# Inverses by blocks of 16 with corrections on TensorE, and 104 weight chunks split during the first feed-forward

## The chip, the cores and the metric

The kernel runs on one core of one Trainium2 chip. The metric is the device time of one execution in microseconds (us). Three executions of the kernel before took 2127.75, 2129.2 and 2129.91 us; the median is 2129.2 us.

## What is computed

One layer of a hybrid decoder for 264 tokens: 256 of a prompt and 8 single tokens of running sequences. D is 2048, the feed-forward width F is 5504.

```python
x = x + 0.5 * swiglu(rmsnorm(x, n1), f1g, f1u, f1d)      # first feed-forward
h = rmsnorm(x, nm)
proj = h @ w_in                                           # 2048 -> 4864 columns
o_att = attend(q, k, v, sinks)                            # 16 heads, window 128, sinks, relative bias
o_rwkv = rwkv_time_mix(proj[..., ATT_COLS:], ...)         # 16 heads of 64
x = x + concatenate([o_att, o_rwkv]) @ w_out
x = x + 0.5 * swiglu(rmsnorm(x, n2), f2g, f2u, f2d)      # second feed-forward
```

The time mixing is a recurrence over tokens with a 64x64 state S per head:

```python
sa = einsum('bhij,bhj->bhi', S, -kk_t)
S = S * exp(lw_t) + sa[..., None] * (kk_t * a_t) + v_t[..., None] * k_t
y_t = einsum('bhij,bhj->bhi', S, r_t)
```

The kernel computes it for the prompt in four chunks of 64 tokens. Within a chunk it needs, for each head, the inverse of a unit triangular 64x64 matrix I - L, with L strictly triangular. 16 heads times 4 chunks make 64 such inverses. All is float32.

## The kernel before

**Weights.** Every large product is computed as three fp32r products. A weight w is split into hi (w rounded to fp32r) and lo = w - hi, the activation likewise; hi·xh, hi·xl and lo·xh are added in PSUM. `gemm` (L126) walks over a product's rows in chunks of four blocks of 128x128. `chunk` (L115) loads a chunk (256 KB) into one of 6 `raw` buffers from SP's queue (L121), rounds it on ScalarE into one of 4 `hi` buffers (L122), and subtracts on VectorE into one of 4 `lo` buffers (L123, recorded as L57); of w_in the chunk with k0 = 8 is subtracted on GpSimd. Then TensorE runs 12 matmuls of 128x128 by 264 (L73, into the PSUM tiles `acc`). A function `step` is called after each chunk.

**Stages.** The first feed-forward has 43 column tiles in six parts; each part runs its gate and up products, then its share of the down product. Its last part writes x to DRAM (`xsp`) and begins the next norm. The mixing stage follows: 38 tiles of w_in (48 matmuls each, 1824 in all, `win`), tiny products between them, then w_out (768 matmuls). The second feed-forward is built like the first. The feed-forwards have 6192 weight matmuls each.

**Small work in the mixing stage.** It is written as Python generators in a list `tasks`; `tick` (the `step` of w_in and w_out) moves each one to its next `yield`. A scheduler then orders the instructions of every engine by its own estimate; SP's queue, ScalarE's and the others each run in the order so written. The generators:

- `prep`, one for each of 8 pairs of heads: decays, normed keys, and the masked products `gm` (L423) that hold L; 8 stores a batch, of 128-byte rows, bring the two diagonal 32x32 blocks of each L to DRAM (`sa`, L426).
- `chain`, one for each of 4 batches of 2 pairs (16 inverses). It loads the 32 diagonal blocks in two forms (`X`, and `Xt`, rows shared out over 4 groups of 32 partitions; L475, L476, 8 transfers), runs 30 elimination steps of two VectorE instructions each (L486, L487), stores the result to DRAM (`sb`, L491, 4 transfers), loads it in its final layout (`TT`, L496, 4 transfers), adds the identity and transposes (L503, L506), and fills the off-diagonal 32x32 block by two rounds of 16 products of 32x32 on TensorE (L513, L524). Then come the products with `kr` (L538), with `W` (L551), the three steps of the state over the chunks (L575 to L592), a group norm and the output gate.
- `attend`, one for each of 8 query tiles: scores, softmax, transposes (L730 to L732), products with v.
- `dec_rwkv`, the recurrence of the 8 single tokens, in 16 slices of four head rows, with GpSimd and VectorE; `dec_attend`, their attention.

**Order of w_out.** `PASS` (L39) gives the passes over the rows of w_out: pairs 0 to 5 of the time mixing first, then the eight attention tiles, then pairs 6 and 7. `need` drains the generators that a pass waits for; any pass with a time-mixing pair also waits for the single tokens' recurrence. In the last pass each finished tile of x is also split and squared for the next norm.

The rules of the buffers: 3 `acc` and 5 `m` tiles in PSUM; TT in 2 buffers, X and Xt in 1 each.

Of the kernel before, what the change touches and what calls it, by code (L numbers as in the profile page):

```python
# [32 lines left out]
DWAIT = (8, 8, 8, 4)  # L33
# [13 lines left out]
def body(tc, I, O):  # L47
# [42 lines left out]
    def pause(n):  # L90
        for _ in range(n):
            yield

    with ExitStack() as ctx:
# [20 lines left out]
        def chunk(src, n, e, ahead=True):  # L115
            w = n * P
            with tc.high_priority() if ahead else nullcontext():
                raw = wp.tile([P, CH * P], F32, tag="raw", bufs=NRAW, name=uid("raw"))
                hi = wp.tile([P, CH * P], F32R, tag="hi", bufs=NHL, name=uid("hi"))
                lo = wp.tile([P, CH * P], F32R, tag="lo", bufs=NHL, name=uid("lo"))  # L120
                SP.dma_start(raw[:, :w], src)  # L121
                A.copy(hi[:, :w], raw[:, :w])  # L122
                tt(e, lo[:, :w], raw[:, :w], hi[:, :w].bitcast(F32), ALU.subtract)  # L123
            return hi, lo

        def gemm(ps, src, xs, step=None, rng=None, pool=False, ahead=True):  # L126
            n = len(xs)
            for k0 in range(0, n, CH):
# [3 lines left out]
                hi, lo = chunk(src[:, k0 * P:k1 * P], k1 - k0, G if pool and k0 in LOP else V, ahead)  # L132
# [6 lines left out]
                if step:  # L139
                    step()  # L140

# [47 lines left out]
        def early(pi):  # L189
            keep = tc.keep_in_program_order  # L190
            if pi == 1:
                keep(A.dma_start(C, I["cst"]))
                keep(A.dma_start(ss, I["shs"]))
            elif pi in (2, 3):
                nm, ck = (("ks", "ck"), ("vs", "cv"))[pi - 2]
                keep(A.dma_start(O[nm][:, 0:127, :], I[ck][:, 1:128, :]))
# [67 lines left out]
        def first_ffn(n2):  # L264
# [11 lines left out]
            with tc.tile_pool(name="f1", bufs=1) as fp:  # L276
                cur[0] = (fp, NH)
                for q in range(4):
# [3 lines left out]
                    xr += [xg[:, j] for j in range(4)]  # L282
                ffn(n1, xr, I["gu1"], I["dn1"], nxt, load)

# [5 lines left out]
        def mixing_body(mx, n2, n3):  # L290
# [27 lines left out]
            scr = [dp.tile([BATCH[b] * 16, 1024], F32, tag=f"sa{b}", name=f"sa{b}") for b in range(nbat)]  # L318
            scr2 = [dp.tile([BATCH[b] * 16, 1024], F32, tag=f"sb{b}", name=f"sb{b}") for b in range(nbat)]
# [3 lines left out]
            def win(t):  # L323
                ps = acc()
                gemm(ps, I["win"][t], n2.xs, tick, pool=True)
# [25 lines left out]
            def prep(p, bt, k, xrr, xk, xv):  # L351
# [64 lines left out]
                for h in range(2):  # L416
# [7 lines left out]
                    for blk in range(2):  # L424
                        x = blk * 32
                        SP.dma_start(  # L426
                            scr[bt.i].rearrange("(h b k c) (s t) -> h b k s c t", h=2, b=2, c=4, s=32)[h, blk, k],
                            gm[h * 64 + x:h * 64 + x + 32, :, x:x + 32])
# [34 lines left out]
            def chain(bt):  # L463
# [3 lines left out]
                nr = n * 16  # L467
                ng = P // nr
                if ng == 3:
                    ng = 2  # L470
                nj = 32 // ng
                X = ring((ng * nr, 32, 32), "X", 1)
                Y = ring((ng * nr, nj, 32), "Xt", 1)
                for g in range(ng):
                    SP.dma_start(X[g * nr:(g + 1) * nr], scr[bt.i].rearrange("r (s t) -> r s t", s=32))  # L475
                    SP.dma_start(Y[g * nr:(g + 1) * nr],  # L476
                                 scr[bt.i].rearrange("r (j g t) -> g r j t", g=ng, t=32)[g])
                TT = ring((P, n * 4, 64), "TT", NTT)
                for h in range(2):
                    G.memset(TT[h * 64 + 32:h * 64 + 64, :, 0:32], 0.0)  # L480
                yield from pause(DWAIT[bt.i])
                for s in range(1, 31):
                    m, w = -(-s // ng), 31 - s
                    t = ring((ng * nr, m, w), "st", 2)
                    shp = (ng * nr, m, w)
                    tt(V, t, bc(X[:, s:s + 1, s + 1:], shp), bc(Y[:, :m, s:s + 1], shp), ALU.mult)  # L486
                    tt(V, Y[:, :m, s + 1:], Y[:, :m, s + 1:], t, ALU.add)  # L487
                    if s % NSTEP == 0:
                        yield
                for g in range(ng):  # L490
                    SP.dma_start(scr2[bt.i].rearrange("r (j g t) -> g r j t", g=ng, t=32)[g], Y[g * nr:(g + 1) * nr])  # L491
                yield from pause(1)
                for h in range(2):
                    for blk in range(2):
                        x = h * 64 + blk * 32
                        SP.dma_start(TT[x:x + 32, :, blk * 32:blk * 32 + 32],  # L496
                                     scr2[bt.i].rearrange("(h b m) (s t) -> h b s m t", h=2, b=2, s=32)[h, blk])
                yield from pause(DWAIT[bt.i])
                for h in range(2):
                    for blk in range(2):  # L500
                        x = h * 64 + blk * 32
                        v = TT[x:x + 32, :, blk * 32:blk * 32 + 32]
                        tt(V, v, v, bc(ident[x:x + 32, x:x + 32].unsqueeze(1), (32, n * 4, 32)), ALU.add)  # L503
# [508 lines left out]
```

## Time and profile before

| what | value |
|---|---|
| median of three executions | 2129.2 us (2127.75 to 2129.91) |
| the profiled execution | 2127.34 us, of which its span is 2125.2 us |
| TensorE busy over the span | 2043.9 us, 96% |
| VectorE, ScalarE, GpSimd busy | 1334.3, 1045.8, 419.5 us |
| moved by DMA | 356.27 MB, mean 168 GB/s |
| split of a chunk: ScalarE round, VectorE subtract | 602 ns, 684 ns (means over all) |
| first matmul of w_in to first of w_out | about 764 to 1244 us |

Times in the profile are counted from the span's start. A busy TensorE is not TensorE at its peak: matmuls overlap, so 166 weight matmuls fit in 20 us at the full clock although one is shown with 286 ns. The best measure of the loss is therefore the number of weight matmuls in a stretch beside 166 per 20 us. "PEclk" is the share of the full TensorE clock that was granted. An idle time is put down to the event that ended it.

### The profile page before, as it was taken

Reading aid. Unit: us, or ns where it says so; the run is one execution under the profiler, and the core shown is the slowest. Engines: PE = TensorE matmul, PEld = TensorE weight load, DVE = VectorE, ACT = ScalarE, POOL = GpSimd, SP = SyncE. Lnnn points to the kernel's source line nnn. Section 1 sums busy time; section 2 is a strip of 40 time slices with the busy share of each in tenths; the row PEclk is TensorE's granted clock in tenths of the full one; section 3 lists DMA queues with packets and bytes.
Section 4 is the critical chain, followed back from the end, with each engine's and each line's share of the span. In section 5 each row is a group of like instructions: output and inputs, shape, how many; then the busy total and the mean of one; then the engine's idle time right before and its main releaser. Section 6 shows DMA issues by size and latency. Waiting matters only on the chain.

```text
span 2125.2 us, 45168 instructions
## 1 busy us (share of the span) xinstructions
PE 2043.9 (96%) x16870; PEld 1995.4 (94%) x16870; DVE 1334.3 (63%) x2551; ACT 1045.8 (49%) x2002; POOL 419.5 (20%) x581
## 2 busy tenths in 40 slices
PE   8999999999999999989996899999999999999997
PEld 8999999999999999888885679899999999999997
DVE  5765555556555677766888646755555565555555
ACT  5644444444444566546542344644444444444445
POOL 0301011010201146533454201220110102011012
PEclk9999999999999999989997579999999999999999
DMA  6565565656555574434343145456555565555554
GB/s 224 176 182 182 175 205 175 207 180 183 181 177 185 185 227 139 122 96 135 112 136 114 41 138 186 156 182 181 181 175 187 177 184 181 177 186 176 186 176 140
DMA packets 227532, 356.27 MB, mean 168 GB/s; under 512 B 42176, under 2 KB 83152, under 8 KB 227280
## 3 DMA queue, kind: packets, MB, share of 16 engines
q1 hardware_dynamic: 221616, 344.72, 51.8%
q10 hardware_dynamic: 5696, 8.66, 1.1%
q8 instruction: 132, 2.16, 0.4%
q14 instruction: 88, 0.72, 0.1%
HBM read 345.15 MB, written 10.21 MB: 167 GB/s over the span
## 4 chain that ended last, share of the span: by engine, by line
PE 86%; DVE 7%; DMA 2%; ACT 1%; issue 1%; POOL 1%; SPq 1%; DVEq 0%; POOLq 0%; ACTq 0%
PE acc L73 79%; PE m L73 6%; DVE lo L57 1%; DMA raw<-in_gu 1%; DVE Xt L57 1%; DVE st L57 1%; ACT L67 1%; DVE ld L57 0%; ACT t L67 0%; DMA sb<-Xt 0%; DVE s L60 0%; DVE t L57 0%; DMA TT<-sb 0%; DVE TT L57 0%; DVE t L64 0%
## 5 line engine op out<-in xcount | busy, mean ns | idle before, releaser
L73 PE MATMUL acc<-s,hi 128*128 128x264 f32 x7072 | 1317.5, 286 | 10.0 <-ACT hi L122 8.3
L57 DVE TENSOR_TENSOR lo<-raw,hi 128x512 fp32r<-128x512 f32 (+1 forms) x1266 | 861.7, 684 | 600.6 <-ACT hi L122 578.7
L122 ACT CAST hi<-raw 128x512 fp32r<-128x512 f32 (+2 forms) x1304 | 780.5, 602 | 909.5 <-PE acc L73 830.6
L73 PEld LDWEIGHTS acc<-s,hi 128*128 128x128 f32 x7072 | 1108.8, 190 | 17.8 <-ACT hi L122 8.5
L73 PE MATMUL acc<-s,lo 128*128 128x264 f32 x3536 | 1016.1, 288 | 12.7 <-DVE lo L57 10.5
L73 PEld LDWEIGHTS acc<-s,lo 128*128 128x128 f32 x3536 | 669.9, 189 | 18.5 <-DVE lo L57 14.1
L73 PE MATMUL acc<-t,hi 128*128 128x264 f32 x2752 | 502.7, 284 | 1.6 <-ACT t L251 1.6
L73 PEld LDWEIGHTS acc<-t,hi 128*128 128x128 f32 x2752 | 426.0, 188 | 1.9 <-ACT t L251 1.8
L57 POOL TENSOR_TENSOR t<-t,t 128x264 f32<-128x264 f32 (+1 forms) x162 | 173.0, 1068 | 1209.6 <-ACT hi L122 897.6
L73 PE MATMUL acc<-t,lo 128*128 128x264 f32 x1376 | 388.2, 284 | 0.0
L73 PEld LDWEIGHTS acc<-t,lo 128*128 128x128 f32 x1376 | 258.2, 188 | 0.0
L57 DVE TENSOR_TENSOR t<-acc,t 128x264 f32<-128x264 f32 x164 | 70.9, 433 | 36.7 <-PE acc L73 36.5
L57 POOL TENSOR_TENSOR s<-s,s 128x264 f32<-128x264 f32 (+1 forms) x56 | 49.5, 886 | 195.8 <-ACT s L67 179.1
L57 POOL TENSOR_TENSOR lo<-raw,hi 128x512 fp32r<-128x512 f32 x38 | 49.7, 1308 | 57.4 <-ACT hi L122 57.2
L67 ACT ACT_TABLE_LOAD x42 | 53.9, 1283 | 1.9 <-PEq L1004 1.2
L60 DVE SCALAR_TENSOR_TENSOR s<-acc,s 128x264 f32<-128x264 f32 x96 | 40.7, 428 | 16.8 <-PE acc L73 16.3
L60 DVE SCALAR_TENSOR_TENSOR x<-acc,x 128x264 f32<-128x264 f32 x96 | 40.6, 427 | 10.9 <-PE acc L73 10.4
L57 DVE TENSOR_TENSOR st<-X,Xt 128x60 f32<-128x60 f32 (+10 forms) x120 | 36.1, 300 | 10.1 <-DMA Xt<-sa 7.4
L67 ACT ACTIVATE t<-t 128x264 f32<-128x264 f32 x94 | 40.0, 425 | 3.3 <-DVE t L57 1.8
L57 DVE TENSOR_TENSOR Xt<-Xt,st 128x60 f32<-128x60 f32 (+10 forms) x120 | 36.7, 305 | 1.7
L251 ACT CAST t<-t 128x264 fp32r<-128x264 f32 x86 | 35.5, 413 | 3.6 <-POOL t L57 2.1
L73 PE MATMUL m<-s,hi 128*128 128x264 f32 x160 | 30.1, 287 | 0.4 <-ACT hi L122 0.4
(209 smaller groups left out, 1116.5 us busy)
## 6 DMA issues: line engine op xcount, KB each, us to landing
raw<-in_gu SPq DMA_DIRECT2D x688, 256.0 KB, 3.2
raw<-in_dn SPq DMA_DIRECT2D x224, 256.0 KB, 2.7
raw<-in_win SPq DMA_DIRECT2D x152, 256.0 KB, 3.2
raw<-in_dn SPq DMA_DIRECT2D x160, 192.0 KB, 2.7
raw<-in_wout SPq DMA_DIRECT2D x48, 256.0 KB, 3.0
raw<-in_wout SPq DMA_DIRECT2D x32, 128.0 KB, 2.4
xsp<-x ACTq DMA_DIRECT2D x16, 132.0 KB, 3.5
s<-xsp SPq DMA_DIRECT2D x16, 132.0 KB, 3.0
```

Of the source, the lines that this page charges most:

```text
L57: return e.tensor_tensor(out=out, in0=a, in1=b, op=op)
L60: return V.scalar_tensor_tensor(out=out, in0=a, scalar=s, in1=b, op0=op0, op1=op1)
L67: return A.activation(out=out, in_=in_, func=f, **k)
L73: TE.matmul(out, lhsT, rhs, start=start, stop=stop, **k)
L122: A.copy(hi[:, :w], raw[:, :w])
L251: A.copy(hi, u)
```

## The change

Three things change.

1. **The inverse by blocks of 16.** `gm` is stored to DRAM as whole 64x64 matrices (256-byte rows, one transfer for each pair and half, 4 a batch). The chain loads only the four 16x16 blocks on the diagonal, 64 blocks on 64 partitions, by one transfer of 64-byte rows; it runs 14 elimination steps, stores the blocks back by one transfer into a scratch that was filled with zeros during the first feed-forward, and loads 64x64 matrices U that hold the block-diagonal inverse. Two corrections on TensorE make the full inverse: with W the transpose, F = 2I - W + (low·W), U becomes F·U, and again (five rounds of 16 products of 64x64 in place of two of 32x32).
2. **Weights split ahead.** During the first feed-forward a side task splits 104 chunks, one for every four chunks of the feed-forward's own: the chunks k0 = 0, 4 and 12 of the 24 time-mixing tiles of w_in (72), and the second chunk of each tile and pass of w_out (32). Each is loaded (256 KB), rounded, subtracted, and stored to DRAM as hi and lo beside each other (512 KB, from ScalarE's queue). In the mixing stage such a chunk is loaded whole (512 KB) straight into a buffer for hi and lo, and neither ScalarE nor VectorE touches it.
3. **The passes of w_out** become two: the eight time-mixing pairs, then the eight attention tiles. hi and lo share one buffer of twice the size, 4 of them, as before.

The core of the diff:

```diff
-DWAIT = (8, 8, 8, 4)
+DWAIT = (4, 4)
+PRE, PREK = range(2, 26), (0, 4, 12)
+PSTEP = 4
-PASS = [[0, 1, 2, 3, 4, 5], [8, 9, 10, 11, 12, 13, 14, 15], [6, 7]]
+PASS = [[0, 1, 2, 3, 4, 5, 6, 7], [8, 9, 10, 11, 12, 13, 14, 15]]
...
-        def chunk(src, n, e, ahead=True):
+        def chunk(src, n, e, ahead=True, done=None):
...
+                hl = wp.tile([P, 2, CH * P], F32R, tag="hl", bufs=NHL, name=uid("hl"))
+                hi, lo = hl[:, 0], hl[:, 1]
+                if done is not None:
+                    SP.dma_start(hl[:, :, :w].bitcast(F32), done)
+                else:
+                    raw = wp.tile([P, CH * P], F32, tag="raw", bufs=NRAW, name=uid("raw"))
+                    SP.dma_start(raw[:, :w], src)
+                    A.copy(hi[:, :w], raw[:, :w])
+                    tt(e, lo[:, :w], raw[:, :w], hi[:, :w].bitcast(F32), ALU.subtract)
...
+        def presplit(fp):
+            todo = [("win", t, k, CH) for t in PRE for k in PREK]
+            k0 = 0
+            for ks in PASS:
+                if len(ks) > CH:
+                    todo += [("wout", o, k0 + CH, len(ks) - CH) for o in range(KD)]
+                k0 += len(ks)
+            for i, (nm, t, k, n) in enumerate(todo):
+                w = n * P
+                raw = fp.tile([P, CH * P], F32, tag="praw", bufs=3, name=uid("praw"))
+                hl = fp.tile([P, 2, CH * P], F32R, tag="phl", bufs=3, name=uid("phl"))
+                tc.keep_in_program_order(SP.dma_start(raw[:, :w], I[nm][t, :, k * P:k * P + w]))
+                A.copy(hl[:, 0, :w], raw[:, :w])
+                tt(V, hl[:, 1, :w], raw[:, :w], hl[:, 0, :w].bitcast(F32), ALU.subtract)
+                d = dp.tile([P, 2, w], F32, tag=f"pre{i}", name=f"pre{i}")
+                A.dma_start(d, hl[:, :, :w].bitcast(F32))
+                ready[nm, t, k] = d
+                yield from pause(PSTEP)
...
+                for g in side:
+                    next(g, None)
...
+                X = ring((nr, 16, 16), "X", 2)
...
+                SP.dma_start(X, diag(scr[bt.i]))
+                yield from pause(DWAIT[0])
+                G.memset(X.rearrange("r s t -> r (s t)")[:, 0:256:17], 1.0)
+                for s in range(1, 15):
+                    w = 15 - s
+                    t = ring((nr, s, w), "st", 2)
+                    tt(V, t, bc(X[:, s:s + 1, s + 1:], (nr, s, w)), bc(X[:, :s, s:s + 1], (nr, s, w)), ALU.mult)
+                    tt(V, X[:, :s, s + 1:], X[:, :s, s + 1:], t, ALU.add)
...
+                SP.dma_start(diag(scr2[bt.i]), X)
...
+                for h in range(2):
+                    SP.dma_start(U[HALF[h]], scr2[bt.i][h * nj:(h + 1) * nj, 0:4096].rearrange("j (s t) -> s j t", s=64))
+                yield from pause(DWAIT[1])
+                V.transpose(W, U)
...
+                for last in (False, True):
+                    ps = times(low, W)
+                    F = square("F", 1)
+                    stt(F, W, -1.0, bc(I2.unsqueeze(1), (P, nj, 64)), ALU.mult, ALU.add)
+                    tt(V, F, ps, F, ALU.add)
+                    yield
+                    pu = times(part(F), U)
+                    if not last:
+                        pw = times(part(U), F)
+                        W = square("Wt", 1)
+                        A.copy(W, pw)
+                    U = square("U")
+                    V.tensor_copy(U, pu) if last else A.copy(U, pu)
+                    yield
+                TT = U
```

Here `low` reads `gm` and `times` runs 16 products of 64x64 by 64 into one PSUM tile. In the changed program's instruction order TensorE's 1824 matmuls of w_in still stand ahead of those of w_out, in the same sequence. What stands between them differs: the first correction product of batch 3 stands behind 1776 of them (before: the first off-diagonal product of batch 3 stood behind all 1824), and behind the last of them stand only the end of the state steps, the group norm, and the same attention products as before.

More of the change, by code (lines that the diff above doesn't have):

```diff
@@ L466, in chain @@
                     yield
[L467 to L487, printed above, removed]
+                nr, nj = n * 32, n * 4
```

94 lines of the change are left out of this document (41 added, 53 removed).

## The prediction

> **What bounds the kernel now.** I read the 40 slices of the page first, then busy times by stage, then TensorE's waits, then its timeline.
>
> ```profile
> PE   8999999999999999989996899999999999999997
> DVE  5765555556555677766888646755555565555555
> PEclk9999999999999999989997579999999999999999
> DMA  6565565656555574434343145456555565555554
> ```
>
> Both feed-forwards are full at full clock; their own work cannot get faster here. All slack is in slices 15 to 26, the mixing stage. By stage (columns: busy us and instructions of PE, its weight loads, DVE, ACT, POOL; granted clock; DMA share; GB/s):
>
> ```profile
> 8.00:14.00 6.00, 5.63 (x30) 5.30 (x31) 3.54 (x7) 2.60 (x6) 0.00 (x0) 1.00 1.03 410
> 100.00:700.00 600.00, 598.22 (x4916) 597.53 (x4915) 345.67 (x587) 281.35 (x495) 61.48 (x57) 1.00 0.58 185
> ...
> 1340.00:1362.00 22.00, 18.70 (x132) 16.48 (x131) 22.00 (x45) 19.23 (x50) 12.01 (x14) 1.00 0.50 160
> ```
>
> ```profile
> 764.00:1147.00 383.00, 354.51 (x3173) 332.06 (x3171) 298.03 (x667) 203.18 (x423) 193.14 (x331) 0.96 0.46 133
> 1147.00:1199.00 52.00, 33.55 (x303) 27.74 (x302) 31.63 (x100) 10.27 (x37) 13.61 (x20) 0.62 0.19 53
> 1199.00:1244.00 45.00, 37.57 (x136) 24.17 (x136) 27.82 (x107) 24.68 (x75) 6.03 (x17) 0.58 0.29 83
> 1244.00:1362.00 118.00, 114.51 (x941) 109.97 (x941) 78.36 (x159) 61.06 (x133) 18.04 (x28) 0.97 0.52 163
> ```
>
> The last weight matmul of w_in starts at 1147, the first of w_out at 1244: 97 us without one. In the first 52 of them batch 3's inverse ends alone, at a clock of 0.62; the other 45 are attention tiles. At 740 to 764 DMA already runs at a share of 0.82 and 241 GB/s beside a full TensorE.
>
> TensorE's waits in 764 to 1147, then in 1147 to 1244:
>
> ```profile
> PE acc L73 <- DVE lo L57: 9.2, 8, 3.1
> PE m L73 <- DVE gm L57: 5.3, 4, 3.1
> ```
>
> ```profile
> PE m L73 <- DVE TN L506: 12.4, 1, 12.4
> PE m L730 <- DVE t L64: 5.0, 3, 2.9
> ```
>
> VectorE is behind all four: 298 of 383 us busy, with the inverses and the weights in one queue.
>
> **The stage 764 to 1147, taken apart.** 166 weight matmuls fit in 20 us, 121 ns each (page, slices at 100%), so w_in's 1824 cost 221. The tiny products cost 104 (sum over the timeline of the time to the next start, less waits). 58 are left: 28 in listed waits, 30 in a low clock and stretched gaps.
>
> **The change, part by part.**
>
> *Splits during the first feed-forward.* 104 subtractions at 684 ns are 71 us of VectorE, 104 roundings at 602 ns and 104 issues at 330 ns (the xsp stores' row) 97 us of ScalarE. They run beside the first 416 of its 536 chunks, 588 us of TensorE. VectorE goes from 58% to 70%, ScalarE from 47% to 63%: hidden by the four chunks that lie ready. DMA is the tight one: those 416 chunks are 105.9 MB, and 104 times 768 KB add 81.8, in all 187.7 MB in 588 us, 319 GB/s. The trace has 410 GB/s at 8 to 14 us, with 2 KB rows on SP's queue beside ScalarE's. So 78% of that: I take no stall there, but +4 us for the start, where loads bind until 16 us and two more of 256 KB stand in SP's queue. Bounds: 0, and +48 if 295 GB/s (752 to 754 us, share 1.00, mixed with xsp stores) is all that DMA gives. The zero fill, 1.1 MB and eight issues, is 3 us of DMA at 410 GB/s and hidden alike.
> The Trainium skill ("DMA: Bandwidth & Descriptors", Specifications) puts the HBM limit of a core at about 358 GB/s; the 410 here is above it, and even at 358 the 319 would pass.
>
> *The chain.* Per batch go 60 steps (72.8 us over four, 18.2 each), 4 additions and 2 transposes (2.9 us), 16 SP transfers of some 0.55 us issue, 8 gm stores. There come 28 steps on 56 elements or fewer: 0.16 us (8 elements) to 0.33 (60), I take 0.25, 7 us; a transpose of 512 elements (two of 256: 0.86), two F operations of 0.69 each twice and one copy (0.6): 4.2 us. TensorE gives back two rounds at 1.04 us for five of 64x64. These are in no row; 48 of that shape by W, below, start within 2.4 us, 0.8 for 16, at most 1.4 like uv,t:
>
> ```profile
> 932.90 0.33 PE L73 MATMUL m<-t,W 64*64 64x64 f32 x2
> ...
> 935.30 1.37 PE L73 MATMUL m<-uv,t 128*64 128x64 f32 x29
> ```
>
> +2 us a batch, bounds 0 and +5. The new transfers of 1024 rows of 64 B: Xt's 1024 rows of 128 B take four issues of 0.56 and land in 2.8, so 5 us there and 5 back; bounds 2.5 and 10 each. From gm to the first correction: gm 0.7, store 2.5, X 5.4, steps 10.5 (half again for what lies between), back 5.1, U 3.2, transpose 0.9: 28 us. In the changed order 178 weight matmuls (21.6) and about 8 us of tiny products stand there, 30 us. So batches 0 to 2 are barely covered; late next are these transfers.
> The Trainium skill (same page, Specifications) says that below 512 B a transfer is read, modified and written; if that doubled the 64-byte stores it would add 5 us a batch, inside my bound of 10, while the 128-byte stores here land in 2.7 us.
>
> *w_in with ready chunks.* 72 of 152 subtractions leave VectorE (796 ns here, 57 us); with the steps (some 45 less) and the 4.2 us items it falls from 298 to about 200 of 380 us. The 9.2 and 5.3 us above go, and most of the clock dips. A new wait comes in: a ready chunk is loaded into one of only 4 buffers, freed three chunks ahead (4.36 us at full rate), where raw had 6 more; SP stops on that buffer with the chain's transfers queued behind it. Landing of 512 KB is not shown: 16 KB land in 2.1 us, 256 KB in 3.2, so 4.3 by that slope plus 0.3 issue; bounds 3.2 and 7.8 (528 KB of x in the crowded start). At 4.6, 0.24 us for each four chunks, hidden in w_in behind the tiny products (some 3 us a tile). Batch 3's inverse and two attention halves move into this stage: 35 us of tiny products at a clock of 0.62 are about 22 at full, and the corrections 8. So 221 + 104 + 30 = 355, plus what is left of 58: I take 30 (bounds 10 and 60). 385 us, +2.
>
> *The tail.* Behind the last w_in matmul now stand two state steps, norm and gate (5 us), and the 45 us of attention, same instructions. What is new there: the single tokens' recurrence starts 210 weight matmuls before the end (before: 326) and needs 16 times four GpSimd operations of 0.8, 52 us, so it ends about 12 us into the tail, on VectorE too: +5. 97 becomes 55, -42 (bounds 40 and 75).
>
> *w_out.* 768 at 121 ns are 93 of 118. The old last pass of two blocks gives 0.73 us of matmul a tile and VectorE 1.5: full for 22 us while TensorE started 132 of 181. With eight blocks, 2.9 us a tile, that 6 us goes. Waits for ready chunks 16 times 0.24: +4, of which I take +2 as a raw chunk lies between. Net -4.
>
> **The sum.** +4 +2 -42 -4 = -40. The profiled execution (2125.2 us span, 2.1 around it) is 1.9 us below the median; 2127.3 - 40 = 2087.3, and 2129.2 - 40 = 2089 for the median, which I predict.
>
> **The rivals.**
>
> *TensorE stays fed and warm.* If the stage w_in keeps only 10 of its 58 us and the tail runs at full clock, 36 us of tiny products at 0.58 become 21: -20 -15, 2054. For it: VectorE at half load. Against: the tail's attention halves wait on each other (5.0 us) and table loads at any clock.
> The Trainium skill ("TensorE: Matmul & The Clock Gate", What's actually happening) says the clock halves after an idle window of 3.4 us and returns after a busy one; the 12.4 us wait ahead of the clock of 0.62 agrees. By that rule a tail entered without such a gap would stay warm, which is this rival.
>
> *Ready chunks come late.* If 512 KB land in 6 us, each four chunks of w_out lose 1.6: 16 times, 26, and in w_in 24 tiles some 0.6, 14: 2129, nothing gained. For it: SP's queue stops in order and the chain's waits sit in it. Against: 3.2 us for 256 KB at 185 GB/s.
>
> *DMA binds in the first feed-forward, slower.* 187.7 MB in 588 us needs 319 GB/s. The gain of 44 elsewhere is lost at 187.7 MB in 632 us: below 297 GB/s it is a loss. At 285 GB/s, 659 us, +71 in place of the +4: 2156; at 295, 2133. For it: 276 to 295 GB/s at shares near 1 at 750 to 756. Against: there 1 KB rows; stores here are 4 KB rows, like the 410.
>
> *It doesn't do what it says*: the inverse gets shorter, but batch 3 still ends behind w_in, because the order is a scheduler's estimate and the transfers are longer: 25 us of the 42 are lost, 2114. For it: 28 us against 30 of cover.
>
> **How the numbers follow.** Forecast (2070 to 2106) 0.46; fed and warm 0.19; chain still exposed 0.11; ready chunks late 0.11 (half slower than no change); DMA binds 0.13. A measurement of this kernel can tell 0.2% (4 us) from no change. Faster: 0.46 + 0.19 + 0.11 + 0.03 + 0.02 = 0.81; within: 0.05; slower: 0.14. The range takes in the late chunks and most of the warm case: 2046 to 2134; it leaves out the worse DMA rates and the best of the warm case.
>
> **What would show it.** Right: TensorE full up to 760 at a DMA share of 0.8 to 0.95 and above 310 GB/s; the first w_out matmul near 1205; VectorE near half busy in w_in; no wait on TN; TensorE not idle in w_out's last pass. Wrong: waits of ScalarE for raw before 600 us with a share of 1 (DMA binds); TensorE waiting for DMA of hl (late chunks); TensorE waiting for the transpose of U or for F for many us (chain).

## The result, and the profile after

The changed kernel takes 2197.82 us (2185.66 to 2199.13, four runs) beside 2128.94 for the kernel before on the same chip: a ratio of 1.0308, 95% interval 1.0282 to 1.0333. It is slower by 3%. The prediction, 2089 us (2046 to 2134, slower 0.14), was wrong.

The profiled executions differ by 70.4 us (2197.73 and 2127.34). Three marks show where: the first product of the norm behind the first feed-forward, the first product of the norm behind the mixing stage, and TensorE's stretches without weight matmuls between them.

| us | before | after | difference | predicted |
|---|---|---|---|---|
| first feed-forward, to the first mark | 773.4 | 841.9 | +68.5 | +4 |
| first mark to the last weight matmul of w_in | 373.6 | 419.2 | +45.6 | +2 |
| from there to the first of w_out | 97.2 | 58.0 | -39.2 | -42 |
| w_out, to the second mark | 120.5 | 117.5 | -3.0 | -4 |
| mixing, the three together | 591.3 | 594.7 | +3.4 | -44 |

So the tail and w_out came as forecast, and two terms did not. The slices of the changed kernel:

```profile
PE   8989999999999999999998679999999999999997
DVE  5765566666656673445567763566666665656655
PEclk9999999999999999999999759999999999999999
DMA  9879889898986567656434336855556555555554
```

TensorE looks as full in the first 15 slices as before: the digits cut at 90% hide the loss. VectorE now has a dip to 3 and 4 (slices 16 to 18, where 72 splits are gone from w_in) and then 7 again in slices 22 and 23, just where TensorE has its hole (8 and 6; the 7 behind them is the tail). By stage, in the columns shown before:

```profile
100.00:700.00 600.00, 569.38 (x4437) 556.57 (x4438) 369.19 (x625) 291.61 (x540) 48.73 (x55) 0.97 0.86 286
832.00:1215.00 383.00, 358.60 (x3395) 335.18 (x3393) 208.57 (x429) 156.26 (x330) 173.25 (x312) 0.96 0.57 175
1215.00:1240.00 25.00, 13.17 (x178) 11.92 (x180) 14.52 (x39) 2.97 (x9) 8.94 (x12) 0.63 0.20 54
1240.00:1262.00 22.00, 20.61 (x268) 18.05 (x266) 19.16 (x59) 6.58 (x24) 9.99 (x14) 1.00 0.34 98
1262.00:1320.00 58.00, 45.07 (x163) 29.43 (x159) 40.29 (x149) 28.00 (x93) 15.33 (x29) 0.58 0.31 90
1320.00:1437.00 117.00, 116.42 (x985) 114.25 (x985) 54.10 (x103) 41.41 (x88) 17.61 (x28) 0.98 0.73 235
```

In 100 to 700 us, 4437 matmuls stand where 4916 stood: a tenth fewer. VectorE is down to 209 of 383 us in w_in, as forecast, and w_out needs 54 us of it where it needed 78. But ahead of the last part of w_in (1240 to 1262) there is now a hole at a clock of 0.63, and the tail behind it still runs at 0.58, though the clock was 1.00 just before.

TensorE's waits from 830 to 1440 us (us in total, times, longest), then ScalarE's from 100 to 600:

```profile
PE m L75 <- DVE Wt L531: 21.4, 2, 19.5
PE m L765 <- DVE t L66: 10.4, 5, 5.1
PE acc L75 <- DMA hl<-pre: 5.2, 6, 2.0
```

```profile
ACT phl L146 <- DMA praw<-in_win: 102.4, 48, 4.8
...
ACT phl L146 <- DMA praw<-in_wout: 33.2, 21, 5.0
```

Most of the first is one wait of 19.5 us for the transpose of batch 3's U (batch 3 is the last of the four). The second is new: in the first feed-forward ScalarE stands 136 of 500 us at the rounding of a split-ahead chunk (L146) whose load has not landed.

### The profile page after: what moved, and what is told of

The parts are those of the page before. It is cut to its first block, busy times and chain, and to the rows that moved or that the text cites. A ratio compares the mean times of both kernels' runs of the same rounds, so it can differ in the third digit from the quotient of the medians.

```text
span 2195.9 us, 45540 instructions
## 1 busy us (share of the span) xinstructions
PE 2086.0 (95%) x17254; PEld 2024.8 (92%) x17254; DVE 1321.3 (60%) x2391; ACT 1020.6 (46%) x1976; POOL 376.3 (17%) x580
## 4 chain that ended last, share of the span: by engine, by line
PE 72%; DMA 14%; DVE 7%; ACT 3%; issue 2%; POOL 1%; SPq 0%; ACTq 0%; DVEq 0%; POOLq 0%
PE acc L75 63%; PE m L75 8%; DMA praw<-in_win 6%; DMA praw<-in_wout 3%; DVE hl L59 2%; DMA raw<-in_gu 1%; DMA hl<-pre 1%; ACT phl L146 1%; ACT hl L127 1%; DVE t L59 1%; DMA raw<-in_win 1%; ACT L69 1%; POOL t L59 0%; DVE X L59 0%; DVE ld L59 0%
## 5 line engine op out<-in xcount | busy, mean ns | idle before, releaser
L75 PE MATMUL acc<-s,hl 128*128 128x264 f32 x10608 | 1353.9, 288 | 41.0 <-ACT hl L127 23.1
L75 PEld LDWEIGHTS acc<-s,hl 128*128 128x128 f32 x10608 | 1320.3, 190 | 60.6 <-ACT hl L127 26.3
L59 DVE TENSOR_TENSOR hl<-raw,hl 128x512 fp32r<-128x512 f32 x1146 | 810.4, 714 | 459.8 <-ACT hl L127 451.3
L127 ACT CAST hl<-raw 128x512 fp32r<-128x512 f32 (+1 forms) x1184 | 708.4, 605 | 732.3 <-PE acc L75 602.5
L75 PE MATMUL acc<-t,hl 128*128 128x264 f32 x4128 | 519.9, 287 | 16.3 <-ACT hl L127 10.5
L75 PEld LDWEIGHTS acc<-t,hl 128*128 128x128 f32 x4128 | 512.8, 191 | 22.2 <-ACT hl L127 12.8
L59 POOL TENSOR_TENSOR t<-t,t 128x264 f32<-128x264 f32 (+1 forms) x162 | 133.2, 822 | 1298.2 <-DVE t L59 991.6
L59 DVE TENSOR_TENSOR phl<-praw,phl 128x512 fp32r<-128x512 f32 x104 | 73.5, 707 | 152.2 <-ACT phl L146 150.0
L146 ACT CAST phl<-praw 128x512 fp32r<-128x512 f32 x104 | 64.5, 620 | 171.4 <-DMA praw<-in_win 113.1
L59 POOL TENSOR_TENSOR hl<-raw,hl 128x512 fp32r<-128x512 f32 x38 | 49.5, 1303 | 113.7 <-ACT hl L127 112.1
L59 DVE TENSOR_TENSOR pj<-acc,rs 128x264 f32<-128x264 f32 x26 | 11.0, 425 | 45.3 <-PE acc L75 45.2
```

The source lines that it names most:

```text
L59: return e.tensor_tensor(out=out, in0=a, in1=b, op=op)
L75: TE.matmul(out, lhsT, rhs, start=start, stop=stop, **k)
L146: A.copy(hl[:, 0, :w], raw[:, :w])
```

## The experiments: the first feed-forward

Theories: **R**, DMA's rate binds, as my rival said; **L**, a split-ahead load comes too late for its use; **O**, order: the scheduler placed the rounding of a split-ahead chunk ahead of roundings whose data had been loaded earlier, and ScalarE, which runs in order, holds these back. For the mixing, **V**: VectorE is too full at the end of w_in for batch 3's steps.

**e1_no_split**: the changed kernel without any chunk split ahead.

```diff
-                side.append(presplit(fp))
...
-                for _ in side.pop():
-                    pass
```

> The changed kernel without the 104 split-ahead chunks (all chunks are loaded and split where they are used); inverse by 16, two passes of w_out and the shared buffer stay. Marker for the end of the first feed-forward: the first product of ones with the squares (773 us before, 842 in the changed kernel); for the mixing stage the time from there to the same product of the next norm (591 before, 595 changed). Theory R (rate: DMA gives about 300 GB/s) and theory L (a line on ScalarE): both 772 to 776 for the first marker. For the mixing stage, theory V (batch 3's steps share VectorE's queue with the single tokens' recurrence, so the shorter inverse gains nothing and the ready chunks little): 590 to 605. Rival W (the ready chunks' own loads hold the stage back and hide the inverse's gain): 560 to 575. Total by V 2120 to 2140, by W 2095 to 2110.

Measured: 2134.30 us, ratio 1.0019 [1.0010, 1.0028]; first mark 775.0, mixing 594.1. Of the 68.5 us, 66.9 hang on the splits. And the rest of the change, without them, gains nothing in the mixing either.

**e3_lead2**: each split-ahead load is issued two turns earlier, into four buffers.

```diff
+            for i in range(LEAD):
+                fetch(i)
...
+                fetch(i + LEAD)
+                raw = raws.pop(i)
```

> The changed kernel with the load of each chunk to be split ahead issued two turns earlier (4 buffers for it, was 3), so that it has landed long before ScalarE comes to its rounding. Same bytes, same number of instructions. Theory R (DMA cannot give more than about 300 GB/s in this mix of loads and stores): first marker stays at 835 to 845, total 2190 to 2200. Theory L (ScalarE's queue stands still until the load lands, and the feed-forward's own roundings stand behind it): the waits of ScalarE for that load (136 us in 100 to 600) go, the DMA rate rises to 315 GB/s or more, first marker 775 to 795, total 2130 to 2150.

Measured: 2185.54, 1.0268 [1.0245, 1.0292]; first mark 831.1; ScalarE's waits for the loads are still 86 and 38 us. Neither theory's number. The instruction order says why: counting, for each split-ahead chunk, the feed-forward chunks that were loaded before it but are rounded after it gives 2.04 on average in the changed kernel and 1.88 here; the scheduler moved the rounding forward along with the load.

**e4_small_store**: 16 KB of each chunk are stored instead of 512, and the mixing splits all its chunks itself.

```diff
-                A.dma_start(d, hl[:, :, :w].bitcast(F32))
-                ready[nm, t, k] = d
+                A.dma_start(d, hl[:, :, :16].bitcast(F32))
```

> The changed kernel with the store of each split-ahead chunk cut to 16 KB (it was 512 KB), and the chunks split again where they are used, as without the split. Left out: the storing of the split weights; output unaffected. Theory R: 230 GB/s are wanted, no stall is left, first marker 772 to 785. Theory L: the rounding still waits for its load, which lands in some 4 to 5 us in place of 5.7, first marker 800 to 835.

**e5_pstep5**: a chunk for every five of the feed-forward's in place of four (`PSTEP = 5`).

> The changed kernel with one split-ahead chunk for every five chunks of the feed-forward in place of four, so that the 104 are spread over 520 of its 536 chunks (289 GB/s wanted in place of 319). Theory R (cap of about 300 GB/s): first marker 772 to 790, total 2130 to 2145. Theory L (each of the 104 costs its own wait): first marker 825 to 845, total 2180 to 2200.

Both wanted fewer bytes in the same time. R expected the loss to go and L expected it not to grow; both lost more: 2306.87 (one run, first mark 948.2) and 2254.90, 1.0588 [1.0568, 1.0608] (first mark 902.2). The stretch 100 to 600 us of the store cut short, and ScalarE's longest wait in it:

```profile
100.00:600.00 500.00, 428.69 (x3094) 406.45 (x3093) 251.02 (x438) 203.85 (x383) 37.87 (x43) 0.94 0.64 181
```

```profile
ACT phl L146 <- DMA praw<-in_win: 189.7, 55, 7.1
```

181 GB/s at a share of 0.64, and the worst time of all. Theory R is dead. The count of overtaken chunks orders the runs: 1.88, 2.04, 2.62, 3.46 with first marks 831, 842, 902, 948 (and e2 below, 2.16 with 850).

**f2_lead_pin** and **f1_pin**: rounding and subtraction are held in the order in which the program issues them, so that nothing is overtaken (the count is 0 and 0.03); f2 with the earlier load, f1 without.

```diff
-                A.copy(hl[:, 0, :w], raw[:, :w])
-                tt(V, hl[:, 1, :w], raw[:, :w], hl[:, 0, :w].bitcast(F32), ALU.subtract)
+                keep = tc.keep_in_program_order
+                keep(A.copy(hl[:, 0, :w], raw[:, :w]))
+                keep(tt(V, hl[:, 1, :w], raw[:, :w], hl[:, 0, :w].bitcast(F32), ALU.subtract))
```

> The load two turns earlier as in the run before, and the rounding, subtraction and store of the split-ahead chunks held in program order, so that none of them stands on ScalarE ahead of a rounding whose load was issued earlier (on ScalarE such a rounding stands ahead of 2.0 earlier loads on average in the changed kernel, 1.9 with the load two turns earlier, 2.6 with one for every five chunks, 3.5 with the small store). Same bytes as the changed kernel. Theory O (the overtaking costs, as ScalarE stands still for a load while older ones lie ready): with 0 overtaken the first feed-forward is full, first marker 774 to 785, DMA 315 GB/s, total 2128 to 2145. Rival D (DMA's landing time under 320 GB/s starves TensorE anyway): first marker 810 to 845, total 2165 to 2200.

> The changed kernel with the rounding, subtraction and store of the split-ahead chunks held in program order, and the load not earlier. Theory O: with nothing overtaken the loss is mostly gone even so; the rounding still waits for its own load, but behind all older loads: first marker 785 to 805, total 2138 to 2160. Rival (the earlier load is what helps): 825 to 842, total 2180 to 2198.

Measured: f2 2142.38, 1.0066 [1.0042, 1.0090], first mark 786.9; f1 2132.59 (one run), first mark 783.9. Both rivals (first marks of 810 and 825 or more) fell. Theory O holds, though the marks lie 2 us above its range in f2 and 1 us below it in f1; the earlier load of f2 brings nothing. (Only rounding and subtraction are held; the issue of the store is not.) f1's stretch 100 to 600 and ScalarE's first wait in it:

```profile
100.00:600.00 500.00, 493.72 (x4043) 492.01 (x4043) 344.27 (x571) 275.41 (x497) 39.70 (x50) 1.00 0.94 323
```

```profile
ACT hl L127 <- PE acc L75: 129.7, 170, 2.6
```

The same work and the same bytes, and the waits for split-ahead loads are down from 136 us to 3; ScalarE now waits for TensorE, that is, it is ahead of it. 58 of the 68.5 us were order by f1, 55 by f2. How one such wait looks, in ScalarE's timeline of the changed kernel (start, duration; in brackets the idle time before it and what ended it):

```profile
303.55 0.62 ACT L146 CAST phl<-praw 128x512 fp32r<-128x512 f32 x1 [1.23 <-DMA praw<-in_win]
304.07 0.62 ACT L127 CAST hl<-raw 128x512 fp32r<-128x512 f32 x1
...
307.60 0.62 ACT L146 CAST phl<-praw 128x512 fp32r<-128x512 f32 x1 [1.75 <-DMA praw<-in_win]
...
308.13 1.03 ACT L127 CAST hl<-raw 128x512 fp32r<-128x512 f32 x2
```

Behind 65 of the 69 waits a rounding for the feed-forward (L127) follows within 0.3 us: its data lay there. These roundings feed TensorE, and they also free the `raw` buffers for which SP's queue waits (177 us in this stretch, for VectorE's subtraction), in which the next split-ahead load stands. So a late rounding makes the next load late. This last step is argued from the timeline and not shown by itself: in f1 SP's queue waits as long for the same buffers (192 us) and nothing is lost.

**h1_late_start** adds to g1, below, that the side task begins 64 chunks later.

> The kernel with late tiles split ahead (2120.6), with the side task begun 64 chunks later, behind the start in which loads bind. Theory: some 6 of the 16 us that the first feed-forward still loses lie at the start: first marker 781 to 786 (790), total 2110 to 2118. Rival (they come from the rounding's place in ScalarE's queue all along): 788 to 792, total 2118 to 2124.

Measured: 2113.84, 0.9935 [0.9922, 0.9947], first mark 778.0 against g1's 789.8: better than expected. Not all of these 12 us are the crowded start: by the first norm product of the feed-forward itself (68.6 us in the kernel before, 73.2 in the changed one, 74.7 in g1, 68.9 in h1) 6 of them are gained, and with the old inverse (h2 to i3, below) the late start was worth 3.3 us (783.0 to 779.7). Where the rest lies is open. In h1 +4.6 over the kernel before is left.

## The experiments: the mixing stage

**e17_nosplit_prio**: e1 with the chain's steps at high priority (one `with tc.high_priority():` around L517's two instructions).

> No split-ahead chunks, and the 28 elimination steps of each batch are given priority over other VectorE work when the order is made. Theory V (batch 3's steps stand between the single tokens' recurrence on VectorE): the first correction of batch 3 comes 350 us or less after the first marker (383 in all runs so far), the 39 us without a weight matmul ahead of the last tile of w_in shrink to 10 or less, the mixing stage to 555 to 575 (594 without priority), total 2095 to 2115. Rival T (the recurrence and the attention after it set the end whatever batch 3 does): the correction comes earlier, but the first matmul of w_out stays at 470 to 480 after the marker, the mixing stage at 588 to 597, total 2125 to 2138.

Measured: 2135.28 (one run), mixing 598.5: no gain. But batch 3's steps took 39.2 us for 12.7 us of their own, where e1 has 39.4: the priority did not free them, so the run decides nothing between V and T.

**e6_no_dec**: 14 of the 16 slices of the single tokens' recurrence are left out (zeros stand for them).

```diff
+                    if k not in (0, 8):
+                        G.memset(yr[:, r], 0.0)
+                        continue
```

> The changed kernel with 14 of the 16 slices of the single tokens' recurrence left out (their output is not written; zeros in its place go on). First feed-forward as in the changed kernel (842). Theory V: without the recurrence in VectorE's queue the first correction of batch 3 comes 345 us or less after the marker, the 39 us are gone, mixing stage 545 to 570. Rival T by the attention alone (the recurrence does not matter): 585 to 595 with the correction at 375 or later. If the correction comes early and w_out still begins at 470 or later, attention is the end.

Measured: 2169.50 (one run), mixing 568.0, at the upper end of V's range; the first correction came at 367 us, between the two theories' numbers, and a hole of 22 us is left. Batch 3's steps took 27.3 us in place of 45.3. The long wait shrinks from 19.5 to

```profile
PE m L75 <- DVE Wt L531: 7.0, 1, 7.0
```

so the recurrence is worth some 27 us of the mixing, 22 of them in waits, but it is not the whole loss. What batch 3's steps stand among on VectorE, in the changed kernel:

```profile
1190.29 0.74 DVE L59 TENSOR_TENSOR st<-X 64x54 f32<-64x54 f32 x1
...
1191.29 0.74 DVE L59 TENSOR_TENSOR X<-X,st 64x54 f32<-64x54 f32 x1
...
1192.28 1.35 DVE L59 TENSOR_TENSOR ld<-ld,XR 128x256 f32<-128x256 f32 x1
...
1193.69 0.67 DVE L59 TENSOR_TENSOR hl<-raw,hl 128x512 fp32r<-128x512 f32 x1
1194.30 0.40 DVE L693 TENSOR_REDUCE yr<-t 128x4 f32<-128x256 f32 x1
```

Between two dependent steps (`st`, `X`) stand the recurrence (`ld`, `yr`) and the subtraction of a weight chunk (`hl`). The 28 steps have 10.9 us of their own and take 45.3 (1173.0 to 1218.1), with VectorE idle for 1.3 of them.

**g1_pre_late**: f2 with the tiles 14 to 37 of w_in split ahead in place of 2 to 25 (`PRE = range(14, 38)`), so that VectorE is freed of subtractions where batch 3's steps run.

> The kernel with the rounding held in program order, but the 72 split-ahead chunks of w_in are those of its last 24 tiles (14 to 37) in place of 2 to 25, so that the subtractions go from the stretch where VectorE is full (batch 3's steps and the recurrence). Theory V (VectorE is full there): some 10 to 20 us of subtractions leave that stretch, first correction of batch 3 at 365 to 378 after the marker (385 there), mixing stage 575 to 588 (594), total 2122 to 2136. Rival P (the stage is set by TensorE's matmuls and the tail alone): 590 to 600, total 2138 to 2148.

Measured: 2120.64, 0.9962 [0.9948, 0.9975]; mixing 574.2 (f2: 594.5), batch 3's steps in 22.5 us, first correction at 361. Rival P fell; V had the direction right, and the gain was a little larger than its range.

**g2_reorder, g4_mix, g4b_mix_pass**: e1 with another sequence of the tiles of w_in (`SEQ`: batch 3's last, or batches between attention tiles), g2 and g4b also with the attention tiles first in `PASS`. They tried whether the tail can be hidden by order alone (theory S).

> The new inverse without split-ahead chunks; the tiles of w_in in another order (batches 0 to 2, keys and values, queries, then batch 3) and the attention pass of w_out ahead of the time-mixing pass. Theory S (the 97 us without weight matmuls are batch 3's inverse, the recurrence and the attention, all behind w_in, with nothing of w_out allowed to run): attention is done beside batch 3's tiles and its 46 us pass of w_out covers the inverse and the recurrence: gaps of 25 to 60 us in all, mixing stage 535 to 570, total 2075 to 2110. Rival B (VectorE's work in the stage is the bound and only moves): gaps of 85 or more, mixing stage 582 to 600, total 2120 to 2140.

> The same mixed order of the tiles of w_in, but the time-mixing pass of w_out first, as in the changed kernel. Theory S: batch 3's inverse and the recurrence still stand ahead of all of w_out; only part of the attention leaves the tail: gaps of 60 to 85 us, mixing stage 560 to 582, total 2100 to 2122. If the order of the passes does not matter (rival B), as the run with the other order of passes.

> As the run before, with the order batches 0, 1, keys and values, batch 2, four queries, batch 3, four queries. Theory S: the attention spreads over a longer stretch, batch 3's inverse starts 23 us of matmuls ahead of the end of w_in and four attention tiles end in the tail: gaps of 20 to 50 us, mixing stage 530 to 565, total 2070 to 2105. Rival B: 582 to 600, total 2120 to 2140.

Measured: 2149.26, 1.0095 [1.0073, 1.0116]; 2144.70 (one run); 2134.09, 1.0026 [1.0014, 1.0038]. Their mixing took 616.8, 609.6 and 595.5 us against e1's 594.1; their stretches of more than 10 us without a weight matmul add up to 123, 141 and 121 us (e1: 105). Theory S fell: the work only gathers elsewhere.

**e2_old_inverse** is the changed kernel with the old inverse (two blocks of 32, 60 steps a batch, `DWAIT = (8, 8, 8, 4)`); **h2_old_inv_late** is g1 with it.

> The changed kernel with the old inverse (blocks of 32, 30 steps) and the split-ahead chunks and passes as changed. Theory V: the longer inverse of batch 3, 18 us of steps in place of 7, costs its difference in the shared queue: first correction of batch 3 at 395 to 410, mixing stage 600 to 615, total 2200 to 2215. Rival (the inverse is not on the path that ends the stage): mixing stage 588 to 597 and total 2190 to 2200.

> The kernel with late tiles split ahead, with the old inverse (blocks of 32) in place of the new. Theory V (VectorE is full around batch 3's inverse, whose 60 steps take 20 us and 28 take 11): first correction of batch 3 at 370 to 382 after the marker (361 with the new inverse), mixing stage 582 to 592 (574), total 2128 to 2138. Rival (as with the changed kernel itself, where the old inverse cost nothing): 568 to 578, total 2114 to 2124.

Measured: e2 2199.89 (one run), first mark 849.7, mixing 588.0 against 594.7, where V had 600 to 615. h2 2091.66, 0.9844 [0.9824, 0.9864], mixing 542.5 against g1's 574.2, below both theories. That contradicts V's expectation: the new inverse *costs* about 30 us here. (The late tiles alone are worth 45.5 us of the mixing with the old inverse, e2 to h2, and 20.3 with the new one, f2 to g1.) Its VectorE work is the shorter one (10.9 against 19.7 us for batch 3), so something else had to pay. Theory **Q** (order): with the new inverse the last preparation of the single tokens stands 1613 weight matmuls into w_in, with the old one 1456. The single tokens start at 325 us behind the first mark instead of 276.

**i1_dwait84** and **i2_dwait168** change only the constant that holds back the chains of the new inverse in h1: `DWAIT = (8, 4)` and `(16, 8)` in place of `(4, 4)`. **i3_old_inv_late_start** is h2 with the late start.

> The run that starts the side task late, with the new inverses, with one constant changed: the chains of the first batches are let go later (DWAIT (8, 4) in place of (4, 4)), so that in the instruction order the last product of the preparation of the single tokens stands after 1474 matmuls of the w_in stage instead of 1614, and its other preparations about 100 matmuls earlier too; the arithmetic is the same. Theory Q (order: with the new inverses the chains' corrections stand ahead of the last preparations, so batch 3 and the single tokens' recurrence begin some 50 us later, and that is what the new inverses lose): the single tokens' first product comes at most 290 us after the first marker (325 before), the mixing takes 545 to 555 us instead of 571.7, total 2087 to 2098. Rival V (the new inverses share a full VectorE with the recurrence, wherever they stand): mixing 566 to 575, total 2107 to 2118.

> The same with DWAIT (16, 8): the last preparation product after 1444 matmuls of the w_in stage, but batch 3's correction after 1824 in place of 1692, behind the last of w_in. Theory Q: the single tokens start as early as in the other run (at most 285 us), and what is gained there is partly lost in the stretch without weight products, which is 10 to 25 us longer than in the run with (8, 4): mixing 555 to 575. Rival V: mixing 566 to 575 and the same stretch as in the run with (8, 4).

> The old inverses with the pinned, late preparation, and the side task beginning 64 chunks later: the late start was worth 11.8 us at the first marker with the new inverses (789.8 to 778.0) and 6.8 us in total. Expected 2082 to 2090, mixing 540 to 546, first marker 773 to 781. If the start has no bearing with the old inverses: 2089 to 2094, marker 783.

Measured: i1 2100.03, 0.9850 [0.9830, 0.9870], mixing 560.2, single tokens at 309.9 us; i2 2111.40, 0.9913 [0.9891, 0.9935], mixing 570.6, at 290.7, its last stretch without weight matmuls 23 us longer than i1's; i3 **2084.47, 0.9787 [0.9766, 0.9808]**, mixing 542.0. i1 missed both: Q wanted 545 to 555, and its rival expected nothing of it. i2 has Q's mixing and Q's longer stretch (its mixing fits the rival too), with the single tokens 6 us later than Q allowed. So order alone is not the cause: it gives 11.5 us (571.7 to 560.2), and 18 stay between i1 and i3. The account of TensorE's time shows these. Each instruction is counted from its start to the next start, less the listed wait; "weights" hold the gaps behind weight matmuls:

| mixing, us | weights | tiny products | of these the corrections | waits | sum |
|---|---|---|---|---|---|
| before | 352.2 | 181.8 | 10.9 | 57.3 | 591.3 |
| after | 350.3 | 193.5 | 31.3 | 50.9 | 594.7 |
| g1 | 345.1 | 191.4 | 33.0 | 37.0 | 574.2 |
| h1 | 346.9 | 187.5 | 30.7 | 37.5 | 571.8 |
| i1 | 353.3 | 180.4 | 28.1 | 26.7 | 560.3 |
| h2 (old inverse) | 343.4 | 162.8 | 8.4 | 35.8 | 542.5 |
| i3 (old inverse) | 348.4 | 160.8 | 8.8 | 32.8 | 542.0 |

i1 and i3 differ by 18.2 us, and their corrections alone by 19.3; h1 and h2 by 29.3 and 22.3. A closer pair is i2 and i3 up to the single tokens' first product: in i2 it stands behind 12 fewer weight matmuls (1444 and 1456) and yet comes 13.6 us later (290.7 and 277.1), and 10.6 of these are corrections (14.7 us up to there, and 4.1). The new inverse moves work from VectorE, which has room after the splits are taken from it (busy 59% of the mixing in h1, 65% in i3), to TensorE, which bounds the stage. This is an account and not an experiment: no run changed the corrections alone, and i1 does not quite reach i3's order (last `gm` of batch 3 at 303 and 274 us behind the first mark). In the changed kernel itself the corrections showed little, because the old inverse there (e2) leaves batch 3's end behind w_in: 93.7 us without a weight matmul, beside 58.0. The groups of the changed kernel, then those of h2 (busy us, mean ns, idle before):

```profile
L75 PE MATMUL m<-U,F 64*64 64x64 f32 x256 | 13.7, 240 | 1.4 <-DVE F L59 0.8 <-DVE stb L737 0.6
L75 PE MATMUL m<-Wt,gm 64*64 64x64 f32 x256 | 13.3, 236 | 21.5 <-DVE Wt L531 21.4
L75 PE MATMUL m<-F,U 64*64 64x64 f32 x128 | 7.2, 248 | 0.0
```

```profile
L76 PE MATMUL m<-TN,gm 32*32 32x32 f32 x128 | 4.7, 192 | 0.0
L76 PE MATMUL m<-TT,zs 32*32 32x32 f32 x128 | 4.4, 192 | 0.0
```

640 matmul records for 256: every product is recorded as two. i3 beats both kernels: it keeps the chunks split ahead, held in order and of w_in's tiles 14 to 37, and the two passes, and drops the new inverse. The stretch of i3 around its tail, 64 us at a clock of 0.74:

```profile
1140.00:1204.00 64.00, 54.18 (x374) 38.89 (x375) 49.19 (x176) 31.96 (x105) 17.67 (x33) 0.74 0.31 90
```

## Why the prediction was wrong

**Splits during the first feed-forward: the step that failed most.** I took +4 and wrote that VectorE's and ScalarE's new work is "hidden by the four chunks that lie ready". It measured +68.5. The loads were right (f1, 100 to 600 us: VectorE 344 of 500, 69% for the 70% forecast; ScalarE 275, 55%, for 63% with the issues in it), but I summed busy time on an engine that runs in order. Four chunks ready are 5.8 us of TensorE (48 matmuls at 121 ns). That covers the work of a rounding (0.6 us), but not 69 waits of up to 5 us in 500 us, each with the feed-forward's own roundings behind it. The step weighed the order of the instructions for TensorE, and not for ScalarE, where it decides. Without the overtaking the term is +10.5 (f1) to +13.5 (f2), with a later start +4.6 (h1). The +4 that I took for the crowded start itself was right: by the first norm product of the feed-forward the changed kernel is 4.6 us late (73.2 and 68.6).

**Rival "DMA binds": right sign, wrong mechanism.** Its sign of being wrong, "waits of ScalarE for raw before 600 us with a share of 1", came with a share of 0.88. That its 285 GB/s and +71 lie near the 286 GB/s (100 to 700 us) and +68.5 measured is luck: the rate was low because ScalarE stood, not because DMA gave no more. f1 moved 323 GB/s with the same bytes, just above the 319 I had needed, for 500 us at a TensorE of 99%. The Trainium skill ("DMA: Bandwidth & Descriptors", Specifications) puts a core's HBM limit at about 358 GB/s; the 323 held for 500 us lie below it, the 413 from 8 to 14 us above.

**The chain: the steps, not the transfers.** The transfers of batch 3 were no worse than taken: X landed in 3.0 us (5), the way back into the scratch and on to SP's next issue took 2.6 (5), U 2.8 (3.2), the transpose 0.71. The steps were the term: 10.5 us taken, 45.3 measured. From the last `gm` (1165.6) to the first correction (1225.4) 60 us passed where I had 28 against a cover of 30. I had priced the steps alone, with half again for what lies between, though in the kernel before batch 3's 60 steps, 20.5 us of their own, took 73.5 us beside the same recurrence and subtractions. The recurrence too was priced by its own work, at 52 us; it took 110 (1175.6 to 1285.5), and 134 in the kernel before. Half the load on average, as it came out, says nothing of the last 45 us. Most of the 45.6 us lost in w_in, where I had +2, is that: the rival "it doesn't do what it says", with a hole of 39 us (35.0 and, 16 weight matmuls later, 4.2) where it had 25. Of this hole 19.5 us are the one wait for Wt; in the rest TensorE does batch 3's corrections and attention products, at a clock of 0.63 from 1215 to 1240. And a shorter chain did not end earlier: from the last `gm` to the first correction it took 92 us in the kernel before and 60 here, but that `gm` came 294 us behind the first mark before and 324 here, so the correction came at 386 and 384. The Trainium skill ("DMA: Bandwidth & Descriptors", Specifications) has transfers below 512 B read, modified and written; that this would double the 64-byte stores, as I weighed, does not show: they landed in 3.2 us (median of four), the 128-byte ones of half the size in the kernel before in 2.7.

**The corrections on TensorE.** I took +2 us a batch, bounds 0 and +5, choosing by 48 products that start within 2.4 us. Measured: 31.3 - 10.9 = 20.4 over four batches, 5.1 each, just above the upper bound. I read 64x64 products as 0.8 us for 16; the timeline of the changed kernel has

```profile
953.09 1.54 PE L75 MATMUL m<-Wt,gm 64*64 64x64 f32 x32
954.56 0.71 PE L75 MATMUL m<-ld,tw 65*128 65x128 f32 x4
```

1.47 us from start to start for a round. The 1.4 of `uv,t`, which I had as the upper bound, was the right row.

**The tail and w_out.** 55 predicted, 58.0 measured; -4 and -3.0. The sizes were right, the tail's in part by luck: the recurrence ended 24 us into it and not 12, but TensorE's product with its result (`yr`) stood so late in the order, at 1302, that it waited for nothing. What I had called a gain of 42 was in fact a move (w_in's stage without the hole is 428 - 39 = 389 us, from 833 to 1261, for the 385 forecast): the hole of batch 3 went from behind the last weight matmul to 48 matmuls ahead of it. The sum priced what moved into w_in as 30 us of work behind a covered inverse, and had no wait in it.

**Fed and warm.** The rival fell: the tail was entered at a clock of 1.00 and ran at 0.58, with waits of up to 5.1 us in it. Within it the mean clock falls from stretch to stretch:

```profile
1262.00:1275.00 13.00, 7.67 (x32) 4.82 (x30) 11.36 (x37) 5.54 (x17) 6.27 (x9) 0.72 0.38 116
1275.00:1290.00 15.00, 9.49 (x38) 6.11 (x35) 12.20 (x38) 6.46 (x24) 3.81 (x6) 0.61 0.24 71
1290.00:1305.00 15.00, 14.79 (x49) 9.80 (x49) 7.24 (x40) 6.15 (x26) 0.00 (x0) 0.50 0.19 53
```

The trace has the clock at 0.50 from 1267.8 to 1278.0 and from 1281.4 to 1325.8, and at 1.00 in the rest of the tail. The first fall came at the end of a wait of 2.8 us, the second in the wait of 5.1. It came back 6.7 us after the first weight matmul of w_out (7.4 us in the kernel before, 5.4 in i3). The Trainium skill ("TensorE: Matmul & The Clock Gate", What's actually happening) has the clock halve after an idle window of about 3.4 us and come back after a busy one. The second fall agrees; the first came behind a shorter wait. From 1290 to 1305 the clock stayed at 0.50 although the trace shows TensorE busy for 14.79 of 15 us, with 49 matmuls; why this did not count as a busy window, no run here tells.

**Ready chunks late.** This rival fell too: 512 KB landed in 4.4 us (4.3 estimated), and TensorE waited 5.2 us in all for them.

**What stays open.** No run changed the attention products in the tail, where the clock was 0.58 to 0.74 in the kernels before, after, i1 and i3. And order (11.5) and corrections (22.3) add to 34 us, 5 more than h1 loses to h2: the two are not quite apart.

## What to carry to other kernels

Work put beside a full engine must be checked in the order of each in-order queue, not by busy shares: count, for each new instruction that waits on a transfer, what older work stands behind it. A shorter dependent chain is worth little where its engine is full at that place, or where the order lets it begin later: read the load of the last stretch, not of the stage. And work should leave the engine that bounds the stage, not move to it, however small its matmuls are.

## What the runs showed of the hardware

- DMA held 310 to 332 GB/s for stretches of 100 us with TensorE at 98 to 100% and the clock at 1.00 (f1, h1, 100 to 500 us): loads of 256 KB, and stores of 512 KB on another queue.
- The first feed-forward was slower at the lower DMA rate: at a share of 0.64 and 181 GB/s it lost 175 us (e4, 948.2 against 773.4), at 0.94 and 323 GB/s 10.5 (f1). DMA's rate was not its limit.
- Each fall of the clock in the tail came at or in a wait of TensorE of 2.8 and 5.1 us, and the clock came back 5.4 to 7.4 us after weight matmuls set in (before, after, i3).
- A load and a store of 1024 rows of 64 bytes cost one issue of 0.6 us each and land in 3.0 and 3.2 us (medians of four each, changed kernel).
- A 64x64x64 product in float32 takes about 92 ns of TensorE (two records; 1.47 us for 16), a 32x32x32 one 70 (8.8 us for 128 of them, i3).
